# The recurrence's level products get a longer planned margin behind the VectorE multiplications that they read

## The chip, the core and the metric

The kernel runs on one core of a Trainium2 chip. The metric is the device time of one execution in microseconds (us), as the median of several executions: 1126.6 us over 3 runs (1125.8 to 1126.96). The engines are named as in the profile: PE is TensorE (its weight loads are PEld), DVE is VectorE, ACT is ScalarE, POOL is GpSimd and SP is SyncE, whose queue issues the DMAs here.

## What is computed

One layer of a streaming encoder, on x of shape (1, 1024, 1024) in float32. Token mixing comes first: RMSNorm with an adaLN shift and scale, one input projection of 3072 columns, a convolution group (gate, causal depthwise convolution over 31 taps, group norm, swish), an HGRN2 group of 4 heads with a gated linear recurrence in chunks of 64, then an output projection, RMSNorm, a gate and the residual. Channel mixing follows: the same norm, an MLP of width 4096 with a squared ReLU, RMSNorm, gate and residual. The recurrence, to which the change belongs, is this:

```python
def step(state, inp):
    qb, kb, vb, lb_ = inp
    cum = jnp.cumsum(lb_, axis=2)
    diff = cum[:, :, :, None, :] - cum[:, :, None, :, :]
    decay = jnp.exp(jnp.where(causal[None, None, :, :, None], diff, -jnp.inf))
    att = jnp.einsum("bhtk,bhsk,bhtsk->bhts", qb, kb, decay)
    o = jnp.einsum("bhts,bhsv->bhtv", att, vb) + \
        jnp.einsum("bhtk,bhkv->bhtv", qb * jnp.exp(cum), state)
    ...
```

The kernel never forms a cumulative logarithm. It builds `att` by levels of doubling block size.

## The kernel before, in words

**Stages.** First the x tiles are normalised and transposed and three column groups of the input projection are multiplied (`pf` on PE). Then the rest of the input projection runs, column group after column group, in the order of the list `ORDER`: the conv gate (`ptG`), the gate of one head (`pj`), the conv value (`ptU`), the recurrence's v (`ptV`), and the other groups of the heads (`pj`). Each group is 48 or, for the transposed ones, 4 times 48 matmuls of 128x512. The output projection (`pout`), the MLP's up projection (`pup`) and its down projection (`al`, `be`) follow. Everything else is laid in between these large products: the heads, the convolution, the modulation vectors.

**A head.** `head_att` goes through seven levels, h = 1, 2, 4 up to 64. At a level PE multiplies blocks of K with blocks of Q into a PSUM tile named `pl` (for h = 1 it sums a prepared product against ones). Then DVE multiplies half of the columns of Q and half of those of K by the decay E of the neighbouring half block, and squares E up, so that Q, K and E fit the next level; the next level's `pl` product reads the new Q and K. After these DVE copies `pl` into the attention tile under a mask (`COPY_PREDICATED`, h up to 8), or ACT copies it (h from 16). There are four heads, so 28 `pl` products. Before the levels come two diagonal products (`pd`), after them transposes (`tn`), state products (`pS`), outputs (`po`) and their transposes (`pot`). The levels of head 0 stand among `ptG`, those of head 1 among `ptU`, those of heads 2 and 3 among the last `pj` and the first `pout`.

**What sets the order.** All instructions are recorded in one program order by a small planner, the class `Weave`. It keeps a planned clock for each engine and adds an assumed cost for each instruction. The large products are the main stream; every other job is a generator that yields the planned moment at which it wants to go on, and the planner resumes it when PE's planned clock has passed that moment. On the chip the planned clocks do not exist: each engine works its instructions off strictly in the recorded order and waits on semaphores. A product that stands too early in PE's order therefore stops all of PE. `after("V")` gives the planned end of DVE's last instruction plus a margin, EXTRA = 0.4 us unless another is given. `split` puts a subtraction on POOL or on DVE, whichever is planned to end sooner, so other planned moments can also move work between these two engines.

**Other names.** `mods_mid` builds modulation vectors: for each it loads eight tiles `in_wada_n` through two or three staging tiles and adds them up on DVE (`SCALAR_TENSOR_TENSOR s<-s,c_act,s`); `ffn_cols` then sums over partitions on PE (`pm`), `gate_rows` likewise (`pg`). `t_val` adds a bias to `ptU` on DVE, multiplies by the gate on POOL and writes the result to memory (`udram`). When all four parts are written, `conv_input` loads `in_toep` and reads `udram` back into the tile `wide`, and `conv_mm` issues the convolution's small products (`cv`, eight groups of 64).

Of the kernel before, what the change touches and what calls it, by code (L numbers as in the profile page):

```python
# [57 lines left out]
AHEAD, RES = 10, 3  # L58


CSTEP = 8
NEAR, EXTRA, LO_G, DLAT, DLAT0 = 1.0, 0.4, 0.5, 2.0, 2.0
XIDLE, HIDLE, WIDLE = 0.3, 0.3, 0.3
XRANK, MRANK, RMODS, RCONV, RLOAD, RNORM = 0, 1, 7, 6, 3.5, 1.5
# [144 lines left out]
class Weave:  # L209
# [30 lines left out]
    def after(self, key, extra=None):  # L240
        return max(self.t[key], self.now) + (EXTRA if extra is None else extra)
# [47 lines left out]
def block_kernel(ctx: ExitStack, tc: tile.TileContext, x, vecs, masks, rows, vrow, crow, wada_t, wada_n,  # L289
# [3 lines left out]
    V = wv.engine(nc.vector, "V", lambda op, n: 0.16 + n / 930)  # L293
# [5 lines left out]
    after, idle = wv.after, wv.idle  # L299
# [12 lines left out]
    def free(tiles):  # L312
        for t in tiles:
            t.release()
# [24 lines left out]
    def ps1(name):  # L339
        return aux.take(psum.tile([P, 512], F32, tag="aux", bufs=2, name=name))  # L340
# [375 lines left out]
    def conv_mm(p, w, toeps):  # L716

        for q in range(2):
            yield acc.free
            ps = acc.take(ps_acc("cv"))  # L720
            for i in range(16):
                m = 16 * q + i
                for c in range(4):
                    for r in range(2):
# [3 lines left out]
                                  start=True, stop=True, us=0.0125)  # L728
                if i % CSTEP == CSTEP - 1:
                    yield wv.now + 0.5  # L730
# [95 lines left out]
    def head_q(j, ps):  # L826
        hd = heads[j]
        yield room(2 + HRES)
        q, Q = hd["q"], hd["Q"] = new(), new()
        A.activation(q.f, ps, AF.Sigmoid, bias=bcol(8 + j))  # L830
        yield after("A")
        V.scalar_tensor_tensor(q.f, ps, bcol(8 + j), q.f, ALU.add, ALU.mult)
        mm.done(ps, "V")
        yield hd["fk"]
        V.tensor_tensor(Q.f, q.f, hd["f"].f, ALU.mult)


        K = hd["K"].f
        yield idle("G", 1.0)
        G.tensor_tensor(q.f, q.f, K, ALU.mult)  # L840
        yield after("G", 0)
        yield room(3 + HRES)
        own = pair()
        prev = new(F32R)
        yield from split(q.f, own[0].r, own[1].r)
        Kv = K.rearrange("p (m s) -> p m s", s=2)
        Qv = Q.f.rearrange("p (m s) -> p m s", s=2)
        yield idle("G", 1.0)
        G.tensor_tensor(q.f[:, H0], Kv[:, :, 0], Qv[:, :, 1], ALU.mult)
        yield after("G", 0)  # L850
        yield from split(q.f[:, H0], prev.r[:, H0], prev.r[:, H1])
        hd["own"], hd["prev"] = own, prev
        q.release()
        wv.add(head_att(j), 1)

    def head_att(j):
        yield lambda: att_turn[0] >= j - 1
        hd = heads[j]
        att = atts[j % 2]
        f, K, Q = (hd[n].f for n in "fKQ")  # L860
        for half in range(2):
            yield aux_free
            pd = ps1("pd")
            for i, t in enumerate(hd["own"]):
                TE.matmul(pd, lhsT=ones_r, rhs=t.r[:, HALF[half]], start=(i == 0), stop=(i == 1))
            yield after("PE", 0.1)
            V.copy_predicated(att[:, half * 4:half * 4 + 4, :],
                              eye_u[:, None, :].broadcast_to([P, 4, P]),
                              pd.rearrange("p (n t) -> p n t", t=P))
            done1(pd, "V")  # L870
        free(hd["own"])
        h = 1
        while h <= 64:
            m = T // (2 * h)
            nb = 64 // h
            Qv = Q.rearrange("p (m s i) -> p m s i", s=2, i=h)
            Kv = K.rearrange("p (m s i) -> p m s i", s=2, i=h)

            Ev = f.rearrange("p (m s i) -> p m s i", s=2, i=h)[:, :, :, 0]
            yield aux_free  # L880
            pl = ps1("pl")
            av = att.rearrange("p n (b s i) -> p n b s i", s=2, i=h)
            Qn = Q.rearrange("p (n b s i) -> p n b s i", n=NT, s=2, i=h)
            plv = pl.rearrange("p (n b i) -> p n b i", n=NT, i=h)
            if h == 1:
                for i in range(2):
                    TE.matmul(pl, lhsT=ones_r, rhs=hd["prev"].r[:, HALF[i]], start=(i == 0), stop=(i == 1))
                hd["prev"].release()
            for n in range(NT if h > 1 else 0):
                if h in MASKED:  # L890
                    for g in range(4):
                        o = g * 32
                        TE.matmul(pl[o:o + 32, n * 16:(n + 1) * 16], lhsT=K[:, n * P + o:n * P + o + 32],
                                  rhs=Qn[:, n, g * nb // 4:(g + 1) * nb // 4, 1, :], start=True, stop=True, us=0.015)
                else:
                    for b in range(nb):
                        o = b * 2 * h
                        TE.matmul(plv[o:o + h, n, b, :], lhsT=K[:, n * P + o:n * P + o + h],
                                  rhs=Qn[:, n, b, 1, :], start=True, stop=True, us=h * 0.001)
            yield after("PE", 0.1)  # L900
            V.tensor_tensor(Qv[:, :, 1, :], Qv[:, :, 1, :],
                            Ev[:, :, 0:1].broadcast_to([P, m, h]), ALU.mult)
            V.tensor_tensor(Kv[:, :, 0, :], Kv[:, :, 0, :],
                            Ev[:, :, 1:2].broadcast_to([P, m, h]), ALU.mult)
            V.tensor_tensor(Ev[:, :, 0], Ev[:, :, 0], Ev[:, :, 1], ALU.mult)
            t = after("V")
            if h in MASKED:
                mk = lev_u[h].rearrange("p (b i) -> p b i", i=h)
                if h == 1:
                    V.copy_predicated(av[:, :, :, 1, :],  # L910
                                      mk[:, None, :, :].broadcast_to([P, NT, nb, h]), plv)
                else:
                    plg = pl[:, 0:P].rearrange("p (n b i) -> p n b i", n=NT, i=h)
                    for g in range(4):
                        o, bs = g * 32, slice(g * nb // 4, (g + 1) * nb // 4)
                        V.copy_predicated(av[o:o + 32, :, bs, 1, :],
                                          mk[o:o + 32, None, bs, :].broadcast_to([32, NT, nb // 4, h]),
                                          plg[o:o + 32])
            else:
                for b in range(nb):  # L920
                    o = b * 2 * h
                    A.activation(av[o:o + h, :, b, 1, :], plv[o:o + h, :, b, :], AF.Copy)
            done1(pl, "V" if h in MASKED else "A")
            yield t
            h *= 2
        hd["att"] = True
        wv.add(head_state(j), 1)
# [49 lines left out]
    def head_state(j):  # L977
        hd = heads[j]
        yield lambda: all(("vh", s) in hd for s in range(4))
        v, f = hd["v"].f, hd["f"].f  # L980
        yield room(2)
        Kn = new()
        yield from to_nat(hd["K"].f, Kn.f)
        hd["K"].release()
        yield room(1)
        hd["S"] = new()
        St = hd["S"].f
        yield after("A")
        for half in range(2):
            yield aux_free  # L990
            pS = ps1("pS")
            for i in range(4):
                n = half * 4 + i
                if n < NT - 1:
                    sl = slice(n * P, (n + 1) * P)
                    TE.matmul(pS[:, i * P:(i + 1) * P], lhsT=Kn.f[:, sl], rhs=v[:, sl], start=True, stop=True)
            yield after("PE", 0.1)
            for i in range(4):
                n = half * 4 + i
                if n < NT - 1:  # L1000
                    sl = slice(n * P, (n + 1) * P)
                    nxt = St[:, (n + 1) * P:(n + 2) * P]
                    psl = pS[:, i * P:(i + 1) * P]
                    if n == 0:
                        V.tensor_copy(nxt, psl)
                    else:
                        V.scalar_tensor_tensor(nxt, St[:, sl], f[:, n * P:n * P + 1], psl, ALU.mult, ALU.add)
            done1(pS, "V")
        Kn.release()
        hd["f"].release()  # L1010
        yield after("V")
        for half in range(2):
            wv.add(head_out(j, half), 2)
# [931 lines left out]
```

## Time and profile before

| what | value |
|---|---|
| median of 3 runs | 1126.6 us |
| the profiled execution, its own time | 1126.3 us |
| its span in the trace | 1124.3 us |
| PE busy | 1083.6 us, 96% of the span |
| DVE busy | 719.3 us, 64% |
| ACT busy | 464.1 us, 41% |
| POOL busy | 299.4 us, 27% |
| mean granted PE clock | 0.992 |

The profiled execution is 2.0 us longer than the span of its trace and 0.3 us shorter than the median. In a row of a timeline stand the start, the duration, the engine, the line and operation, the output and the inputs, and the number of instructions merged into the row; the square bracket gives the time for which the engine stood idle before it and what ended that. Recorded helper lines hide where an instruction was written (all of PE's products have one line), so tiles' names tell the rows apart.

### The profile page before, as it was taken

What the parts mean: (1) busy time and instruction counts of PE and PEld (TensorE: products, weight loads), DVE (VectorE), ACT (ScalarE), POOL (GpSimd) and SP (SyncE); (2) the same over time, 40 slices, a digit from 0 to 9 for tenths busy, and PEclk for the clock granted to TensorE, in tenths of its full rate; (3) what the DMA queues carried; (4) which work ended last, traced back from release to release, by engine and by line L of the source; (5) the groups of instructions that cost most, each with busy time, mean ns of one, the idle gap of its engine ahead of it and who ended that gap; (6) DMA issues with size and microseconds to landing.
All of it is one profiled execution on the core that took longest, in us unless ns stands there. A gap on an engine that the chain in (4) does not pass through costs nothing.

```text
span 1124.3 us, 17080 instructions
## 1 busy us (share of the span) xinstructions
PE 1083.6 (96%) x7036; PEld 880.4 (78%) x7036; DVE 719.3 (64%) x762; ACT 464.1 (41%) x659; POOL 299.4 (27%) x199
## 2 busy tenths in 40 slices
PE   6999998999999989989999999999999999999997
PEld 2787877778877778868888888888888888888886
DVE  3537678238599961766666975333266969997952
ACT  6641311002456433567452334456643334354530
POOL 5121022003373430482101420134400001303511
PEclk8999999999999999999999999999999999999999
DMA  9524433837311402454679745315667957675711
GB/s 365 194 82 132 132 110 120 210 89 191 92 57 39 132 20 75 168 204 171 225 242 341 279 148 187 113 57 179 214 238 268 323 204 243 226 275 176 292 56 75
DMA packets 57101, 195.21 MB, mean 174 GB/s; under 512 B 6208, under 2 KB 10688, under 8 KB 56768
## 3 DMA queue, kind: packets, MB, share of 16 engines
q1 hardware_dynamic: 57024, 194.13, 50.8%
q8 instruction: 55, 0.90, 0.3%
q14 instruction: 22, 0.18, 0.0%
HBM read 158.39 MB, written 35.72 MB: 173 GB/s over the span
## 4 chain that ended last, share of the span: by engine, by line
PE 78%; DVE 8%; DMA 4%; POOL 4%; issue 2%; ACT 2%; SPq 1%; POOLq 0%; DVEq 0%; ACTq 0%
PE pup L1829 26%; PE al L1829 15%; PE be L1829 12%; DVE s L236 7%; PE pout L1829 5%; PE pj L1829 5%; PE ptV L1829 4%; PE pf L1829 3%; DMA s<-in_wada_n 2%; PE ptG L1829 2%; POOL s L236 2%; ACT s L236 1%; PE pm L1829 1%; PE po L1829 1%; PE pl L1829 1%
## 5 line engine op out<-in xcount | busy, mean ns | idle before, releaser
L236 DVE TENSOR_TENSOR s<-s,s 128x1024 fp32r<-128x1024 f32 (+3 forms) x339 | 422.0, 1283 | 84.1 <-ACT s L236 49.9
L236 ACT ACTIVATE s<-s 128x1024 fp32r<-128x1024 f32 (+2 forms) x313 | 300.9, 993 | 346.5 <-DVE s L236 208.4
L236 POOL TENSOR_TENSOR s<-s,s 128x1024 fp32r<-128x1024 f32 (+4 forms) x86 | 198.2, 2312 | 546.1 <-ACT s L236 461.7
L1829 PE MATMUL pup<-s,s 128*128 128x512 f32 x1344 | 308.1, 390 | 0.0
L1829 PEld LDWEIGHTS pup<-s,s 128*128 128x128 f32 x1344 | 251.5, 188 | 51.9
L1829 PE MATMUL al<-s,s 128*128 128x512 f32 x768 | 175.0, 389 | 0.0
L1829 PEld LDWEIGHTS al<-s,s 128*128 128x128 f32 x768 | 144.1, 188 | 30.3 <-DVE s L236 0.4
L1829 PE MATMUL be<-s,s 128*128 128x512 f32 x576 | 131.0, 389 | 0.0
L1829 PEld LDWEIGHTS be<-s,s 128*128 128x128 f32 x576 | 108.1, 188 | 22.5
L1829 PE MATMUL pj<-s,s 128*128 128x512 f32 x432 | 107.4, 397 | 2.2 <-issue 1.5
L1829 PE MATMUL pout<-s,s 128*128 128x512 f32 x384 | 94.9, 401 | 2.0 <-DVE s L236 2.0
L1829 PEld LDWEIGHTS pj<-s,s 128*128 128x128 f32 x432 | 78.9, 188 | 18.4 <-issue 1.7
L1829 PEld LDWEIGHTS pout<-s,s 128*128 128x128 f32 x384 | 71.6, 191 | 17.0 <-DVE s L236 2.4
L236 DVE TENSOR_TENSOR s<-pup,s 128x1024 f32<-128x1024 f32 x24 | 29.3, 1222 | 47.5 <-PE pup L1829 47.3
L236 DVE SCALAR_TENSOR_TENSOR s<-s,c_act,s 128x1024 f32<-128x1024 f32 x28 | 39.5, 1411 | 29.7 <-DMA s<-in_wada_n 29.6
L236 DVE SCALAR_TENSOR_TENSOR s<-pup,s 128x1024 f32<-128x1024 f32 x16 | 19.6, 1225 | 53.3 <-PE pup L1829 50.3
L1829 PE MATMUL ptV<-s,s 128*128 128x512 f32 x192 | 47.4, 407 | 0.0
L1829 PE MATMUL ptU<-s,s 128*128 128x512 f32 x192 | 46.1, 394 | 0.0
L1829 PE MATMUL ptG<-s,s 128*128 128x512 f32 x192 | 45.9, 394 | 0.0
L1829 PEld LDWEIGHTS ptV<-s,s 128*128 128x128 f32 x192 | 37.5, 197 | 8.2
L236 ACT ACTIVATE junk<-s 128x1024 bf16<-128x1024 f32 (+1 forms) x30 | 30.0, 998 | 31.6 <-DVE s L236 24.2
L1829 PEld LDWEIGHTS ptG<-s,s 128*128 128x128 f32 x192 | 35.6, 188 | 7.8 <-ACT s L236 0.3
(126 smaller groups left out, 804.3 us busy)
## 6 DMA issues: line engine op xcount, KB each, us to landing
s<-in_wdn SPq DMA_DIRECT2D x72, 512.0 KB
s<-in_wup SPq DMA_DIRECT2D x56, 512.0 KB
s<-in_wada_n SPq DMA_DIRECT2D x32, 512.0 KB
s<-in_x SPq DMA_DIRECT2D x16, 512.0 KB
s<-in_wada_t SPq DMA_DIRECT2D x16, 512.0 KB
u<-s SPq DMA_DIRECT2D x16, 512.0 KB
s<-u SPq DMA_DIRECT2D x16, 512.0 KB
s<-in_wint SPq DMA_DIRECT2D x12, 512.0 KB
```

The lines of the kernel that those rows point to most:

```text
L236: return op(*a, **k)
L1829: return self.te.matmul(out, lhsT=lhsT, rhs=rhs, **k)
```

## The change

The margin behind the three DVE multiplications of a level becomes a parameter of its own, LEXTRA = 1.0 us, in place of EXTRA = 0.4 us. The moment `t` is what the generator yields at the end of the level, before the next level's product is recorded.

```diff
-CSTEP = 8
+CSTEP, LEXTRA = 8, 1.0
 ...
             V.tensor_tensor(Ev[:, :, 0], Ev[:, :, 0], Ev[:, :, 1], ALU.mult)
-            t = after("V")
+            t = after("V", LEXTRA)
             if h in MASKED:
```

No instruction of the computation is added or removed, but the planner records another order. Three places show how.

On PE, head 1's `pl` products among the `ptU` matmuls (`s_1233` is its Q, `s_693` its K). Each piece of the difference stands at a fixed place of the `ptU` stream.

```order
 L1829 MATMUL ptU<-s_601,s_111 128x512
 L1829 MATMUL ptU<-s_600,s_112 128x512
-L1829 MATMUL pl<-s_1233,s_693 32x16 x32
 L1829 MATMUL ptU<-s_600,s_113 128x512
 L1829 MATMUL ptU<-s_601,s_113 128x512
```

This is the product of h = 2; it goes 6 `ptU` matmuls further back. Counted through, the numbers of `ptU` matmuls from the product of h = 1 to that of h = 2 and so on to h = 64 were 18, 18, 18, 18, 24, 18, and are now 24, 24, 18, 18, 18, 18. Head 0, among `ptG`, had 18, 24, 18, 18, 24, and now has 24, 24, 18, 24, 18 before its last product, which goes 6 back within `pj`.

On DVE, the same head from the masked copy of h = 1 on (`s_1218` or `s_1224` is a modulation vector, `s_1424` or `s_1417` the second of the four parts of the conv value, `s_692` is E). Before:

```order
L236 COPY_PREDICATED s_682<-msk,pl 128x512
L236 SCALAR_TENSOR_TENSOR s_1218<-s_245,c_act,s_1218 128x1024
L236 TENSOR_TENSOR s_1233<-s_1233,s_692 128x256x2
L236 TENSOR_TENSOR s_693<-s_693,s_692 128x256x2
L236 TENSOR_TENSOR s_692<-s_692 128x256
L236 COPY_PREDICATED s_682<-msk,pl 32x8x8x2 x4
L236 TENSOR_TENSOR s_1424<-ptU,s_675 128x1024
L236 TENSOR_TENSOR s_1233<-s_1233,s_692 128x128x4
L236 TENSOR_TENSOR s_693<-s_693,s_692 128x128x4
```

And now:

```order
L236 COPY_PREDICATED s_682<-msk,pl 128x512
L236 SCALAR_TENSOR_TENSOR s_1224<-s_245,c_act,s_1224 128x1024
L236 TENSOR_TENSOR s_1417<-ptU,s_675 128x1024
L236 TENSOR_TENSOR s_1233<-s_1233,s_692 128x256x2
L236 TENSOR_TENSOR s_693<-s_693,s_692 128x256x2
L236 TENSOR_TENSOR s_692<-s_692 128x256
L236 COPY_PREDICATED s_682<-msk,pl 32x8x8x2 x4
L236 SCALAR_TENSOR_TENSOR s_1224<-s_245,c_act,s_1224 128x1024
L236 TENSOR_TENSOR s_1233<-s_1233,s_692 128x128x4
```

The evacuation of `ptU`, after which POOL multiplies by the gate, stood before the multiplications of h = 4 and now stands before those of h = 2. Likewise the last evacuation of `ptU` stood behind head 1's last level and now stands before it.

On PE, the partition sum `pm` of the second modulation vector stood alone among the `ptV` matmuls:

```order
L1829 MATMUL ptV<-s_721,s_105 128x512
L1829 MATMUL ptV<-s_720,s_106 128x512
L1829 MATMUL pm<-ones,s_1218 128x1 x8
L1829 MATMUL ptV<-s_761,s_107 128x512
L1829 MATMUL ptV<-s_762,s_107 128x512
```

Now it stands between the first two groups of the convolution's products:

```order
L1829 MATMUL cv<-wide,s_1724 32x32 x2
L1829 MATMUL cv<-wide,s_1725 32x32 x2
L1829 MATMUL pm<-ones,s_1224 128x1 x8
L1829 MATMUL cv<-wide,s_1722 32x32 x2
L1829 MATMUL cv<-wide,s_1723 32x32 x2
```

The convolution itself moved forward: 168 matmuls (`ptU` 6, `ptV` 162) lay between head 1's last `pl` and the first `cv` group, and now 126 (`ptV` alone). From the first up projection on, PE's order is the same as before.

## The prediction

> **What bounds the kernel now.** I read the page's busy times first, then the waits of PE by what ended them, then PE's timeline around each wait.
>
> ```profile
> span 1124.3 us, 17080 instructions
> PE 1083.6 (96%) x7036; PEld 880.4 (78%) x7036; DVE 719.3 (64%) x762; ACT 464.1 (41%) x659; POOL 299.4 (27%) x199
> ```
>
> PE is busy for 1083.6 of 1124.3 us, and the change adds it no work. What can move is the 40.7 us in which PE stands idle, and the slices in which its clock is low. The largest cause is the one that the change addresses (total us, times, longest):
>
> ```profile
> PE pl L1829 <- DVE s L236: 10.2, 8, 2.7
> ...
> PE cv L1829 <- issue: 2.4, 1, 2.4
> ```
>
> So at most 10.2 us lie in the waits of `pl` themselves, 0.9% of the time. Here they stand one by one for heads 0 and 1, in PE's timeline:
>
> ```profile
> 98.83 0.73 PE L1829 MATMUL pl<-s,s 128*32 128x16 f32 x64 [1.43 <-DVE s L236]
> ...
> 162.32 0.73 PE L1829 MATMUL pl<-s,s 128*32 128x16 f32 x64 [0.22 <-DVE s L236]
> 173.90 0.73 PE L1829 MATMUL pl<-s,s 128*32 128x16 f32 x64 [1.52 <-DVE s L236]
> ...
> 186.82 0.70 PE L1829 MATMUL pl<-s,s 128*32 128x32 f32 x32 [1.58 <-DVE s L236]
> ...
> 191.76 1.15 PE L1829 MATMUL pl<-s,s 128*64 128x64 f32 x16
> ...
> 201.35 1.92 PE L1829 MATMUL pm<-ones,s 128*128 128x1 f32 x16 [1.43 <-DVE s L236]
> ```
>
> Why DVE is late is in its own timeline, beside POOL's:
>
> ```profile
> 96.20 1.28 DVE L236 SCALAR_TENSOR_TENSOR s<-s,c_act,s 128x1024 f32<-128x1024 f32 x1 [3.15 <-DMA s<-in_wada_n]
> ...
> 165.60 1.29 DVE L236 TENSOR_TENSOR s<-s,s 128x512 f32<-128x512 f32 x2
> ...
> 170.30 3.46 DVE L236 TENSOR_TENSOR s<-s,s 128x512 f32<-128x512 f32 x2
> ...
> 170.46 2.75 POOL L236 TENSOR_TENSOR s<-s,s 128x1024 f32<-128x1024 f32 x1 [16.15 <-DVE s L236]
> 183.21 3.46 DVE L236 TENSOR_TENSOR s<-s,s 128x512 f32<-128x512 f32 x2
> 183.38 2.75 POOL L236 TENSOR_TENSOR s<-s,s 128x1024 f32<-128x1024 f32 x1 [10.17 <-DVE s L236]
> 397.32 5.06 DVE L236 TENSOR_TENSOR s<-s,s 128x512 f32<-128x512 f32 x2 [1.48 <-PE pl L1829]
> ```
>
> Two causes. At 98.83 a modulation product waited for its DMA and stood ahead of the multiplications. At 173.90 and 186.82 the pair of multiplications took 3.46 us in place of 1.29, each time with a POOL product beside it, which starts when DVE has evacuated `ptU`.
>
> **The change, term by term.** The price of a PE step comes from a long undisturbed row, and the price of an idle stretch includes what the clock does after it:
>
> ```profile
> 301.84 19.33 PE L1829 MATMUL pj<-s,s 128*128 128x512 f32 x84
> ...
> 204.00:208.00 4.00, 4.00 (x12) 0.57 0.62 175
> ```
>
> A matmul costs 19.33/84 = 0.23 us: 6 are 1.4 us, 18 are 4.1, 24 are 5.5, 126 are 29.0. After the wait and the small products at 201.35 the granted clock (third number from the end of the window's row) was 0.57 for 4 us, which lost 4 x 0.43 = 1.7 us.
>
> *Head 0:* the product of h = 2 goes 6 `ptG` back, 1.4 us of cover for a wait of 1.43. DVE's end is fixed by the DMA, so nearly all goes: -1.4 (from -1.4 to 0).
>
> *Head 1:* 0.22, 1.52 and 1.58 are 3.3 us. The product of h = 2 goes back by 1.4 us. The `ptU` evacuation now stands before the multiplications of h = 2, so the POOL product falls on them: the slow pair now has 24 matmuls and the product's own 0.7 us as cover, 6.2 us, against the evacuation and 3.46 (4.7 us) behind a modulation product. The next slow pair is that of h = 16, with 4.1 + 0.7 us. I leave 0.5 us of waiting: -2.8 (from -3.3 to 0).
>
> *`pm` and the first convolution group:* the wait at 201.35 and its slow clock, 1.4 + 1.7 = 3.1 us, leave their place. But `pm` now stands between two `cv` groups that come 42 matmuls nearer to head 1's last `pl`. Is their input there? The chain before (DVE, then on SP's queue the first loads for the convolution and the last of the four reads into `wide`, two windows with DMA share and GB/s last, and the first `cv`):
>
> ```profile
> 196.44 1.21 DVE L236 TENSOR_TENSOR s<-ptU,s 128x1024 f32<-128x1024 f32 x1
> ...
> 204.77 1.92 SPq L236 DMA_DIRECT2D s<-in_toep  x4
> ...
> 209.03 0.30 SPq L710 DMA_DIRECT2D wide<-udram  x1
> ...
> 228.00:230.00 2.00, 2.00 (x10) 1.67 (x9) 0.00 (x0) 0.45 (x1) 0.00 (x0) 1.00 0.38 150
> 230.00:232.00 2.00, 2.00 (x10) 1.66 (x9) 0.00 (x0) 0.62 (x1) 0.00 (x0) 1.00 0.01 2
> ...
> 236.23 1.52 PE L1829 MATMUL cv<-wide,s 64*32 64x32 f32 x128
> ```
>
> From 196.44 to the end of all these loads it is at most 230 - 196.4 = 33.6 us. The eight loads for the convolution (8 x 512 KB = 4.2 MB) share it with 1 MB issued behind them: 5.2 MB from 204.8 to 230, 0.2 MB per us, by which the eight alone end near 225, or 28 us after 196.4. Now the evacuation stands before head 1's last level and its matmuls end when that level's `pl` starts. In the old clock that is 191.76, less 4.2 gained above, plus 1.4 for the six `ptU` now ahead: 189.0. The input lands between 217 (28 us) and 222.6 (33.6 us); `cv` is asked for at 189.0 + 1.1 + 29.0 = 219.1. PE waits 0 to 3.5 us there, or a little later in `pm`, whose last modulation product needs a tile loaded behind `wide` and 1.3 us of DVE. I take a wait of 2 us and half a slow slice, 0.9: it cancels the 3.1 leaving. Net 0 (from -3.1 to +3).
>
> *Convolution groups closer together:* the second `cv` group of the first pair stopped for 2.4 us (the `issue` row above: PE waited for nothing that the trace shows). In the second half of the convolution the pairs had 6 `pj` and a `po` or `pot` between them; now 6 `pj` alone. Bounds 0 and 2 x 2.4 = 4.9; I take +1.5, nearer to none because another pair with only 6 matmuls between lost next to nothing.
>
> *Heads 2 and 3 and what stands around them:*
>
> ```profile
> 322.23 0.66 PE L1833 MATMUL cpb<-msk,s 128*128 128x128 f32 x4 [1.05 <-DVE s L236]
> 330.61 0.72 PE L1829 MATMUL pd<-s,ones_r 128*128 128x512 f32 x2 [0.85 <-ACT s L236]
> 341.71 0.74 PE L1829 MATMUL pl<-s,s 128*32 128x16 f32 x64 [0.34 <-DVE s L236]
> 366.93 4.37 PE L1829 MATMUL pj<-s,s 128*128 128x512 f32 x18 [0.67 <-DVE s L236]
> 371.60 0.66 PE L1833 MATMUL tn<-msk,s 128*128 128x128 f32 x4 [0.30 <-DVE s L236]
> 385.01 0.74 PE L1829 MATMUL pl<-s,ones_r 128*128 128x512 f32 x2 [1.54 <-DVE s L236]
> 397.93 0.66 PE L1833 MATMUL pot<-msk,s 128*128 128x128 f32 x4 [0.67 <-ACT s L236]
> 404.05 0.73 PE L1829 MATMUL pl<-s,s 128*32 128x16 f32 x64 [2.70 <-DVE s L236]
> ...
> 304.00:404.00 100.00, 91.87 (x838) 73.36 (x836) 91.00 (x119) 52.11 (x94) 53.98 (x25) 1.00 0.22 69
> ```
>
> These waits are 8.1 us. Between head 2's levels stood 12 to 18 `pj` and a few transposes; now 18 to 24. Against that, DVE is busy for 91 of these 100 us (third pair of the last row), and the changed order gives it more: two subtractions of 128x1024 and three of 128x512 go over from POOL, and five of the eight modulation products of `gate_rows` that ran before 301 now come after the last `cv`:
>
> ```profile
> 88.76 1.23 DVE L236 TENSOR_TENSOR s<-s,s 128x1024 fp32r<-128x1024 f32 x1 [3.56 <-ACT s L236]
> ...
> 422.76 0.69 DVE L236 TENSOR_TENSOR s<-mfull,s 128x512 fp32r<-128x512 f32 x1 [1.37 <-ACT s L236]
> ```
>
> That is 2 x 1.23 + 3 x 0.69 + 5 x 1.28 = 10.9 us more for DVE, not all of it inside this stretch; but head 2's levels are spread over 138 `pj` in place of 90 (11 us) and the last `cv` comes 30 matmuls (6.9 us) earlier, so DVE has more time too. Queued behind each modulation product are the next level's multiplications, and PE waits for these. I take half of the waits as gone: -4.0 (from -8.1 to +4, if the extra DVE work shows on PE by a third).
>
> *The last `pot`:* both halves of head 3's outputs now come together right before the final 132 `pout`; half by half there were 12 `pout` between. What follows a `pot` is an evacuation on DVE, a copy on ACT and a subtraction on DVE:
>
> ```profile
> 420.64 0.75 DVE L236 SCALAR_TENSOR_TENSOR mfull<-pot,vec,s 128x512 f32<-128x512 f32 x1
> ...
> 422.11 0.62 ACT L236 ACTIVATE s<-mfull 128x512 fp32r<-128x512 f32 x1
> ```
>
> With the 0.69 us from above that is 2.1 us, of which 6 `pout` hide 1.4: about +0.5 (0 to 2).
>
> Sum: -1.4 - 2.8 + 0 + 1.5 - 4.0 + 0.5 = -6.2 us. The profiled execution took 1126.3 us (span 1124.3 and 2.0 around it), 0.3 below the median of 1126.6. So the median goes to 1126.6 - 6.2 = 1120.4 us.
>
> **The rivals.**
>
> *A. Forecast:* PE's waits shrink by 3 to 9.5 us, 1117 to 1123.5. Chance 0.55.
>
> *B. The slow pairs follow.* If POOL's products beside the multiplications are what counts, a margin of 0.6 us more does not reach the 2.2 us by which they lengthen a pair. The three waits behind such pairs (1.52, 1.58, 2.70: 5.8 us) stay somewhere; the sum is near -0.5, 1126. For it: the rows at 170.30, 183.21 and 397.32. Against it: planned moments fall between whole 6-matmul steps, so many levels got 5.5 us. Chance 0.17. The Trainium skill (SBUF — State Buffer, Who interferes with whom) speaks for this one: a VectorE instruction with two SBUF inputs contends with a GpSimd instruction that reads SBUF, and whichever issues first blocks the other. The rows agree (2.2 us lost beside a POOL product of 2.75).
>
> *C. The convolution waits for its input, slower.* Place: the first `cv` group. If the loads land no earlier than before, at 230, the wait is 230 - 219.1 = 10.9 us, and a slow slice of 1.7 follows, against 3.1 saved: +9.5, in sum +3.3, 1130. It decides from a wait of about 8 us on, where the whole gain is gone. For it: the DMA engines' share is still 0.38 in 228 to 230. Against it: the evacuation moves before the last level. Chance 0.10. On the slow slice, the Trainium skill (TensorE: Matmul & The Clock Gate, What's actually happening) says that the clock halves after an idle window of about 3.4 us that runs freely. By that rule a wait of 2 us need not cost a slice; the trace has both, a slow slice behind 201.35 and none behind the 2.70 us at 404.05.
>
> *D. DVE becomes the bound of heads 2 and 3.* The 10.9 us more do not fit into its 9 idle us: 8.1 stay and 4 come on top; in sum -6.2 + 8 = +1.8, 1128.4. Chance 0.10.
>
> *E. Everything hides:* all of 1.4, 3.3, 3.1 and 8.1 less 1.0 new waits, 1126.6 - 15 = 1112, or half way there, 1115. Chance 0.08.
>
> **How the numbers follow.** A change of this kernel can be told from none at about 0.2%, 2.25 us: below 1124.3 is faster, above 1128.9 slower. A and E are faster, and a little of B: 0.67. The rest of B and half of D are the same: 0.19. C and the other part of D, with a stop that no row names: 0.14. The range takes A whole, B, most of D, and E down to its middle: 1115 to 1128.5.
>
> **What would show it.** In the changed trace the waits of `pl` for DVE should fall from 10.2 us to about 3. The 98.83 wait should be gone, the pairs of 3.46 us still there but under cover. PE should wait up to 2 us at the first `cv` or at `pm`, and a second `cv` of a pair may stop for 2 us. DVE in the 100 us of heads 2 and 3 should be as full as before. I am wrong if the waits of `pl` stay at 8 us or more (B or D), or if `cv` waits 8 us (C), or if a new wait stands where none did, above all at `pd`, `pot` or the first `pout`.

## The result: 0.9% slower, not faster

| | us |
|---|---|
| before, median of 4 runs | 1126.2 (1124.6 to 1127.0) |
| changed, median of 4 runs | 1136.9 (1135.4 to 1139.2) |
| ratio | 1.009, 95% interval 1.0071 to 1.0108 |
| predicted | 1120.4 (1115 to 1128.5) |

The sign of the prediction was wrong and the time lies outside its range. Of the runs further down, low_on_vector has one execution of 1348.2 us at a granted clock of 0.751 among its five, which its ratio leaves out.

The page of the changed kernel, its first lines and then the waits of PE by cause (total us, times, longest):

```profile
span 1137.4 us, 17080 instructions
PE 1090.3 (96%) x7036; PEld 886.2 (78%) x7036; DVE 725.3 (64%) x767; ACT 464.0 (41%) x659; POOL 285.0 (25%) x194
```

```profile
PE pl L1829 <- DVE s L236: 14.5, 9, 4.2
...
PE cv L1829 <- DMA wide<-udram: 4.9, 1, 4.9
...
PE cv L1829 <- issue: 1.0, 1, 1.0
```

PE ran the same 7036 products, but was busy for 6.7 us longer (1090.3 against 1083.6): they ran at a lower clock, 0.982 on the mean against 0.992. The waits of `pl` grew from 10.2 to 14.5 us. The profiled execution is the longest of the changed kernel's four, 2.4 us above their median, so its span shows 13.1 us more where the medians show 10.7. Where the 13.1 us went follows from the first start of a few tiles in both traces, which cut the program at places that both share:

| stretch | before | changed | difference |
|---|---|---|---|
| up to the first `ptV` (heads 0 and 1) | 194.3 | 193.0 | -1.3 |
| (the same from the first `pl` on) | 101.8 | 99.0 | -2.8 |
| first `ptV` to first `tn` (convolution) | 59.2 | 62.2 | +2.9 |
| first `tn` to first `pup` (heads 2 and 3) | 247.1 | 258.8 | +11.7 |
| first `pup` to the end | 623.6 | 623.4 | -0.2 |

Heads 0 and 1 did gain. The third stretch holds the loss; here it is in the view of windows (length, then busy time of PE, PEld, DVE, ACT and POOL, the granted clock, the DMA share and GB/s), before and then changed:

```profile
253.60:500.70 247.10, 233.34 (x2201) 191.94 (x2200) 172.95 (x237) 114.86 (x247) 110.50 (x73) 0.99 0.33 103
```

```profile
255.20:514.00 258.80, 239.27 (x2200) 196.46 (x2199) 176.74 (x238) 114.84 (x247) 100.31 (x69) 0.97 0.31 95
```

PE's idle time rose from 13.8 to 19.5 us (length less busy time), +5.8, and the same products took 5.9 us longer at the lower clock. PE's timeline of the changed kernel names the stops, and windows of 4 us show the clock behind them:

```profile
351.15 1.06 PE L1829 MATMUL pl<-s,s 128*32 128x16 f32 x64 [4.16 <-DVE s L236]
373.12 0.77 PE L1829 MATMUL pl<-s,s 128*32 128x32 f32 x32 [1.90 <-DVE s L236]
384.15 1.22 PE L1829 MATMUL pl<-s,ones_r 128*128 128x512 f32 x2 [3.55 <-DVE s L236]
...
409.14 0.69 PE L1829 MATMUL pl<-s,s 128*16 128x16 f32 x64 [1.51 <-DVE s L236]
```

```profile
348.00:352.00 4.00, 0.85 (x64) 0.88 (x64) 3.71 (x7) 0.18 (x1) 0.26 (x1) 0.71 0.00 0
352.00:356.00 4.00, 4.00 (x24) 3.20 (x17) 3.52 (x6) 0.45 (x1) 0.00 (x0) 0.50 0.18 28
...
372.00:376.00 4.00, 2.88 (x37) 2.48 (x38) 3.97 (x6) 3.26 (x5) 0.53 (x1) 0.70 0.38 125
376.00:380.00 4.00, 4.00 (x17) 3.18 (x17) 4.00 (x3) 2.16 (x3) 4.00 (x2) 0.87 0.47 120
...
384.00:388.00 4.00, 3.85 (x14) 2.87 (x15) 3.69 (x6) 0.00 (x0) 0.00 (x0) 0.59 0.48 142
```

The products that stopped are head 2's h = 4 and h = 32 and head 3's h = 1 and h = 16. Before the change there was one stop among head 2's levels, of 0.34 us. DVE and POOL of the changed kernel show why the first one is late:

```profile
339.78 0.74 DVE L236 SCALAR_TENSOR_TENSOR mfull<-pot,vec,s 128x512 f32<-128x512 f32 x1
341.21 0.69 DVE L236 TENSOR_TENSOR s<-mfull,s 128x512 fp32r<-128x512 f32 x1 [0.70 <-ACT s L236]
343.17 5.64 DVE L236 TENSOR_TENSOR s<-s,s 128x1024 fp32r<-128x1024 f32 x3 [1.26 <-ACT s L236]
...
349.24 1.76 DVE L236 COPY_PREDICATED s<-msk,pl 32x128 f32<-32x128 uint32 x4
...
376.13 5.09 DVE L236 TENSOR_TENSOR s<-s,s 128x512 f32<-128x512 f32 x2
381.14 2.32 DVE L236 TENSOR_TENSOR s<-s 128x16 f32<-128x16 f32 x1
```

```profile
343.59 1.90 POOL L236 TENSOR_SCALAR s<-s 128x1024 f32<-128x1024 f32 x1
345.47 2.79 POOL L236 TENSOR_TENSOR s<-s,s 128x1024 fp32r<-128x1024 f32 x1
...
375.47 7.95 POOL L236 TENSOR_TENSOR s<-s,s 128x1024 fp32r<-128x1024 f32 x3 [3.65 <-ACT s L236]
```

The row at 343.17 merges a low-part subtraction of `split` (128x1024), which waited 1.26 us for ACT, with the two multiplications of h = 2 that are queued behind it. A clean pair takes 1.29 us and the subtraction 1.2, 2.5 in all; these took 5.64, beside two POOL instructions. The masked copy of h = 2, queued behind them, was late by as much: it ended at 351.00, and the product of h = 4 started at 351.15. At 376.13 head 2's last pair took 5.09 us, and the squaring behind it, 128x16, 2.32, both beside three POOL subtractions.

So five theories went to the chip. **H**: the margin in heads 2 and 3 is the loss. **C**: the early convolution is, through what it shifts. **Q**: the place of the multiplications in DVE's queue. **B**: POOL's subtractions beside them. **K**: the clock that each stop lowers.

### The profile page after: what moved, and what is told of

Same layout as the page of the kernel before. It is cut to its first block, busy times and chain, and to the rows that moved or that the text cites. A ratio compares the mean times of both kernels' runs of the same rounds, so it can differ in the third digit from the quotient of the medians.

```text
span 1137.4 us, 17080 instructions
## 1 busy us (share of the span) xinstructions
PE 1090.3 (96%) x7036; PEld 886.2 (78%) x7036; DVE 725.3 (64%) x767; ACT 464.0 (41%) x659; POOL 285.0 (25%) x194
## 4 chain that ended last, share of the span: by engine, by line
PE 76%; DVE 9%; DMA 6%; POOL 4%; ACT 2%; issue 2%; SPq 1%; POOLq 0%; DVEq 0%; ACTq 0%
PE pup L1829 26%; PE al L1829 15%; PE be L1829 11%; DVE s L236 9%; PE pj L1829 5%; PE pout L1829 4%; DMA s<-in_wada_n 4%; PE pf L1829 3%; POOL s L236 2%; PE ptU L1829 2%; PE pm L1829 1%; PE ptV L1829 1%; ACT s L236 1%; PE po L1829 1%; PE pl L1829 1%
## 5 line engine op out<-in xcount | busy, mean ns | idle before, releaser
L236 DVE TENSOR_TENSOR s<-s,s 128x1024 fp32r<-128x1024 f32 (+4 forms) x341 | 428.2, 1293 | 83.0 <-ACT s L236 53.7
L236 POOL TENSOR_TENSOR s<-s,s 128x1024 fp32r<-128x1024 f32 (+4 forms) x84 | 192.8, 2302 | 568.1 <-ACT s L236 456.7
L1829 PE MATMUL pup<-s,s 128*128 128x512 f32 x1344 | 308.1, 390 | 0.0
L1829 PEld LDWEIGHTS pup<-s,s 128*128 128x128 f32 x1344 | 251.6, 188 | 51.8
L1829 PE MATMUL al<-s,s 128*128 128x512 f32 x768 | 175.0, 389 | 0.0
L1829 PEld LDWEIGHTS al<-s,s 128*128 128x128 f32 x768 | 144.1, 188 | 30.3 <-DVE s L236 0.4
L1829 PE MATMUL be<-s,s 128*128 128x512 f32 x576 | 131.0, 389 | 0.0
L1829 PEld LDWEIGHTS be<-s,s 128*128 128x128 f32 x576 | 108.1, 188 | 22.4
L1829 PE MATMUL pj<-s,s 128*128 128x512 f32 x432 | 111.8, 409 | 0.0
L1829 PE MATMUL pout<-s,s 128*128 128x512 f32 x384 | 95.3, 401 | 3.2 <-DVE s L236 2.7
L1829 PEld LDWEIGHTS pj<-s,s 128*128 128x128 f32 x432 | 82.0, 196 | 17.2
L1829 PEld LDWEIGHTS pout<-s,s 128*128 128x128 f32 x384 | 71.5, 191 | 18.7 <-DVE s L236 3.4
L236 DVE SCALAR_TENSOR_TENSOR s<-s,c_act,s 128x1024 f32<-128x1024 f32 x28 | 36.9, 1319 | 32.4 <-DMA s<-in_wada_n 32.2
L1829 PE MATMUL ptV<-s,s 128*128 128x512 f32 x192 | 46.0, 400 | 0.0
L1829 PE MATMUL ptG<-s,s 128*128 128x512 f32 x192 | 45.9, 394 | 0.0
L1829 PE MATMUL ptU<-s,s 128*128 128x512 f32 x192 | 45.7, 393 | 0.0
L1829 PEld LDWEIGHTS ptV<-s,s 128*128 128x128 f32 x192 | 36.7, 193 | 7.9
L1829 PEld LDWEIGHTS ptG<-s,s 128*128 128x128 f32 x192 | 35.6, 188 | 7.7 <-ACT s L236 0.3
```

What stands on the lines that cost most here:

```text
L236: return op(*a, **k)
L1829: return self.te.matmul(out, lhsT=lhsT, rhs=rhs, **k)
```

## The experiments

All times stand against the kernel before, run on the same chip beside them.

| run | median us | ratio to before, 95% interval |
|---|---|---|
| heads01 | 1125.8 | 0.9993 (0.9977 to 1.0010) |
| heads23 | 1128.1 | 1.0016 (0.9998 to 1.0034) |
| conv_hold | 1127.2 | 1.0013 (0.9994 to 1.0031) |
| one_long | 1132.9 | 1.0045 (1.0025 to 1.0066) |
| fill | 1143.6 | 1.0160 (1.0125 to 1.0195) |
| fill_spare | 1133.1 | 1.0068 (1.0046 to 1.0091) |
| no_pool_sub | 1118.2 | 0.9920 (0.9895 to 0.9945) |
| before_no_pool_sub | 1119.6 | 0.9939 (0.9917 to 0.9961) |
| margin12 | 1122.6 | 0.9963 (0.9945 to 0.9981) |
| margin14 | 1123.1 | 0.9971 (0.9957 to 0.9984) |
| low_on_vector | 1120.3 | 0.9939 (0.9919 to 0.9959) |
| m04_low_on_vector | 1121.1 | 0.9951 (0.9930 to 0.9972) |
| m12_low_on_vector | 1115.6 | 0.9906 (0.9883 to 0.9929) |

### Which heads, and the convolution

```diff
-            t = after("V", LEXTRA)
+            t = after("V", LEXTRA if j < 2 else EXTRA)      # heads01
+            t = after("V", EXTRA if j < 2 else LEXTRA)      # heads23
```

```diff
-            yield wv.t["S"] + 2 * DLAT
+            yield wv.t["S"] + 2 * DLAT + (0 if p else 6.0)  # conv_hold
```

> The longer margin stands in heads 0 and 1 alone; heads 2 and 3 are placed with the old 0.4 us. Up to head 2 the order is the changed kernel's, so the convolution still stops for its input (4.90 us) and its clock gap stays. Theory H (the loss comes from where the products of heads 2 and 3 now stand: pl waits of 4.16, 1.90, 3.55 and 1.51 us and the clock gaps behind them): some 10 us better than the changed kernel, 1125 to 1129 us. Rival C (the early convolution shifted everything behind it, and that is what spoils heads 2 and 3): still 1134 to 1138 us, with pl waits over 3 us left.

> The longer margin stands in heads 2 and 3 alone; heads 0 and 1 and the convolution are the kernel's before. Theory H: the loss is here, 1134 to 1138 us. Rival C: the time of before, 1124 to 1128 us, or a little less, because the convolution stands where it stood.

> The changed kernel, with the first convolution asked for 6 us later in the plan, so that 6 us more of ptV stand ahead of it. Theory C: the 4.90 us wait and the half clock behind it (about 5 us) go, and the shift behind it too: 1125 to 1130 us. Theory H: the convolution's own share alone, at most 8 us, if heads 2 and 3 keep their waits: 1129 to 1134 us. Neither holds if the time stays at 1136 us with the wait gone.

heads01 came to 1125.8 us, inside H's range, although its convolution still stopped (first waits of PE, then its third stretch):

```profile
PE pl L1829 <- DVE s L236: 7.9, 8, 3.1
...
PE cv L1829 <- DMA wide<-udram: 3.6, 1, 3.6
```

```profile
251.30:500.60 249.30, 236.45 (x2200) 194.65 (x2199) 174.40 (x239) 115.08 (x247) 97.59 (x68) 0.98 0.31 99
```

249.3 us against 258.8: the loss is in the orders of heads 2 and 3, as H has it, and C falls as the main cause. But heads23, with the long margin only there, lost 1.6 us on the median, not the 8 to 12 that H asked for. And conv_hold, with the long margin everywhere, took 1127.2 us. That lies in the range of C, but not by C's mechanism: its convolution stretch was no shorter (61.9 us; in place of `cv`, a `pm` waited for 4.2 us), while heads 2 and 3, which fell into yet another order, took 248.9. The margin in heads 2 and 3 is thus not bad by itself. Something in the one order that 1.0 us makes there is.

### One swap in VectorE's queue

```diff
-            t = after("V", LEXTRA if j < 2 else EXTRA)
+            t = after("V", LEXTRA if j < 2 or (j, h) == (2, 1) else EXTRA)
```

> The kernel of heads01 (old margin in heads 2 and 3) with the long margin at one place more: after the multiplications of head 2, h=1, so that the product of h=2 is placed 0.6 us later. Nothing else is asked to move, but VectorE's queue then holds the 128x1024 subtraction that waits for ScalarE ahead of the multiplications of h=2 and not behind them. Theory Q (the loss starts at this swap: the multiplications then wait for ScalarE, 1.26 us, for the subtraction, 1.36 us, and run beside GpSimd): the product of h=4 waits 3.5 to 4.5 us as in the changed kernel against 0.35 us in heads01, with a clock gap of some 3 us behind it, and the run takes 5 to 9 us more than heads01, 1130 to 1135 us. Rival N (the loss of heads 2 and 3 is spread over their levels and this one swap is not its start): within 2 us of heads01, 1124 to 1128 us.

The order on DVE against that of heads01, at the place meant (`s_527` is the low part, `s_2952`, `s_2825` and `s_2824` are head 2's Q, K and E):

```
 L236 TENSOR_TENSOR s_2640<-mfull,s_2639 128x512
+L236 TENSOR_TENSOR s_527<-s_775,s_526 128x1024
 L236 TENSOR_TENSOR s_2952<-s_2952,s_2824 128x256x2
 L236 TENSOR_TENSOR s_2825<-s_2825,s_2824 128x256x2
 L236 TENSOR_TENSOR s_2824<-s_2824 128x256
 L236 COPY_PREDICATED s_681<-msk,pl 32x8x8x2 x4
-L236 TENSOR_TENSOR s_527<-s_775,s_526 128x1024
```

DVE's timeline there, in heads01 and then in one_long:

```profile
338.21 0.69 DVE L236 TENSOR_TENSOR s<-mfull,s 128x512 fp32r<-128x512 f32 x1 [0.70 <-ACT s L236]
338.82 1.29 DVE L236 TENSOR_TENSOR s<-s,s 128x512 f32<-128x512 f32 x2
340.02 0.63 DVE L236 TENSOR_TENSOR s<-s 128x256 f32<-128x256 f32 x1
340.56 1.81 DVE L236 COPY_PREDICATED s<-msk,pl 32x128 f32<-32x128 uint32 x4
342.41 1.36 DVE L236 TENSOR_TENSOR s<-s,s 128x1024 fp32r<-128x1024 f32 x1
```

```profile
336.95 0.69 DVE L236 TENSOR_TENSOR s<-mfull,s 128x512 fp32r<-128x512 f32 x1 [0.70 <-ACT s L236]
338.91 5.64 DVE L236 TENSOR_TENSOR s<-s,s 128x1024 fp32r<-128x1024 f32 x3 [1.27 <-ACT s L236]
344.48 0.59 DVE L236 TENSOR_TENSOR s<-s 128x256 f32<-128x256 f32 x1
```

In heads01 the pair starts as soon as DVE is free, takes 1.29 us and is done before POOL's next subtraction begins; the low part comes behind. In one_long the pair stands behind the low part and waits for what that waits for, and then meets POOL: 5.64 us again. The product of h = 4 on PE, in heads01 (where the expectation's 0.35 us belongs to the next product, that of h = 8) and, with the stops that followed, in one_long:

```profile
342.52 0.73 PE L1829 MATMUL pl<-s,s 128*32 128x16 f32 x64 [0.18 <-DVE s L236]
```

```profile
346.90 1.06 PE L1829 MATMUL pl<-s,s 128*32 128x16 f32 x64 [4.19 <-DVE s L236]
367.93 1.07 PE L1829 MATMUL pl<-s,s 128*32 128x32 f32 x32 [3.27 <-DVE s L236]
401.15 0.90 PE L1829 MATMUL pl<-s,s 128*32 128x16 f32 x64 [3.39 <-DVE s L236]
```

It stops for 4.19 us against 0.18. The run took 7.1 us more than heads01 on the medians (5.9 by the ratios, since the kernel before took 0.7 us longer beside it), as Q had asked, and its third stretch took 258.5 us, 9.2 more. N falls. Q as stated is what happened at this place. It is not the whole distance: the planner goes on from another state after the swap, so later rows moved too, and two more stops of over 3 us followed.

### The subtractions on GpSimd

```diff
+            if 1 <= att_turn[0] <= 3:
+                G.memset(lo.bitcast(F32), 0.0)
+            else:
                 G.tensor_tensor(lo, src, hi.bitcast(F32), ALU.subtract)
```

> The changed kernel in the same order on every engine, but from the first product of head 2 to the end of head 3 GpSimd's subtractions that form low parts (11 of 128x1024 and one of 128x512) are memsets to zero, which read nothing: the low parts of these weights and of part of the mix are left out. Theory B (GpSimd beside the level multiplications makes them late: pairs of 4.28 and 5.09 us against 1.29): the pairs take 1.3 to 1.5 us, the waits of 4.16, 1.90 and 3.55 us fall to 1.3, 0.6 and 1 or less, and with the clock gaps behind them 6 to 10 us come back: 1127 to 1131 us. Rival Q alone (the place in VectorE's queue decides, not the contention): the first wait stays at 2.5 us or more and the time at 1133 us or more.

> The control to no_pool_sub: the kernel before, with GpSimd's low-part subtractions from head 2's first product to the end of head 3 made memsets to zero (the low parts are left out). no_pool_sub came to 1118.2 us, 18.6 less than the changed kernel. Theory B (the order of the changed kernel loses because more of its multiplications run beside these subtractions): without them the two orders are about equal, so 1115 to 1121 us here, a gain of 6 to 11 us. Rival Q alone (the loss is the place in VectorE's queue, whatever GpSimd does): the distance between the two orders stays, about 1107 to 1111 us here.

Ten subtractions of 128x1024 and one of 128x512 were replaced in the changed kernel, in an order that is otherwise its own, and ten of 128x1024 and four of 128x512 in the kernel before. Its third stretch without them, then that of the kernel before without them:

```profile
250.70:493.30 242.60, 233.51 (x2200) 192.53 (x2199) 160.72 (x238) 114.72 (x247) 81.68 (x69) 0.99 0.33 102
```

```profile
252.90:496.80 243.90, 234.54 (x2201) 193.27 (x2200) 158.23 (x237) 115.32 (x248) 89.02 (x76) 0.99 0.33 106
```

The two orders are then equal: 242.6 and 243.9 us, 1118.2 and 1119.6 us on the medians. With the subtractions they are 11.7 us apart. So the order loses nothing by itself, and Q alone falls. B holds for the cause; its price was too low, since 18.6 us came back where it had asked for 6 to 10. That POOL itself was late is no rival: PE's only wait for POOL in this stretch is one of 2.04 us at `pt`, in both kernels. One point I had not expected. The subtractions lengthen DVE's work about as much in both kernels: 172.95 - 158.23 = 14.7 us before, 176.74 - 160.72 = 16.0 us in the changed one. Only the price differs: 3.2 us of time before (247.1 against 243.9) and 16.2 in the changed kernel (258.8 against 242.6), in one trace each; on the medians it is 6.5 and 18.6 us. Of the 16.2 us, 10.4 are idle time of PE and 5.8 its busy time at the lower clock.

Groups by shape over the third stretch show which instructions took the delay. The level multiplications before, with the subtractions and without, then the same of the changed kernel with two of its squares of E (L1829 and L1832 are one and the same helper line of PE):

```profile
L236 DVE TENSOR_TENSOR s<-s,s 128x512 f32<-128x512 f32 x28 | 27.0, 1005 | 13.1 <-PE pl L1829 13.0
L236 DVE TENSOR_TENSOR s<-s,s 128x512 f32<-128x512 f32 x28 | 20.3, 766 | 17.5 <-PE pl L1832 17.5
```

```profile
L236 DVE TENSOR_TENSOR s<-s,s 128x512 f32<-128x512 f32 x28 | 30.5, 1132 | 10.0 <-PE pl L1829 10.0
L236 DVE TENSOR_TENSOR s<-s 128x64 f32<-128x64 f32 x2 | 2.7, 1354 | 0.0
L236 DVE TENSOR_TENSOR s<-s 128x16 f32<-128x16 f32 x2 | 2.5, 1251 | 0.0
L236 DVE TENSOR_TENSOR s<-s,s 128x512 f32<-128x512 f32 x28 | 22.4, 840 | 10.7 <-PE pl L1829 10.7
```

The multiplications lost 6.7 us before and 8.1 in the changed kernel. The squares of 128x64 and 128x16 lost 1.1 before (2.0 against 0.9 us) and 4.3 in the changed kernel (5.2 against 0.9). So these steps of the levels, which stand ahead of what PE waits for, lost 7.8 us before and 12.4 in the changed kernel. DVE's own low-part subtractions of 128x1024 turn the other way: they lost 3.2 us before (25.1 against 21.9) and 1.7 in the changed kernel (24.3 against 22.6). This shift of 4.6 us goes the right way and is smaller than the difference in price; that the rest lies in which level had time to spare is argued from the stops and not counted. Without POOL's subtractions the same three instructions as at 343.17 take 3.47 us, and head 2's last pair and its square are clean:

```profile
336.46 3.47 DVE L236 TENSOR_TENSOR s<-s,s 128x1024 fp32r<-128x1024 f32 x3 [1.26 <-ACT s L236]
...
363.77 1.28 DVE L236 TENSOR_TENSOR s<-s,s 128x512 f32<-128x512 f32 x2
364.97 0.18 DVE L236 TENSOR_TENSOR s<-s 128x16 f32<-128x16 f32 x1
...
366.31 1.28 DVE L236 TENSOR_TENSOR s<-s,s 128x512 f32<-128x512 f32 x2
```

The wait for ACT, 1.26 us, is still there; the product of h = 4 then stops for 1.23 us in place of 4.16.

### The clock behind the stops

```diff
+            for _ in range(FILL.get((j, h), 0)):
+                nc.tensor.matmul(pl, lhsT=ones_r, rhs=ones_r[:, None, :].broadcast_to([P, 4, P]),
+                                 start=True, stop=True)      # fill_spare: into an idle bank
```

> The changed kernel in the same order, with matmuls that compute nothing (128x512 on a constant, written to the bank that the real product then overwrites) in the five longest stops: 20 ahead of the first convolution, 16, 7, 14 and 5 ahead of the products of head 2 h=4 and h=32 and head 3 h=1 and h=16. They take the place of the waits and add no time of their own as long as they are shorter than these. Theory K (half of the loss is the clock that each stop lowers; the granted clock cost 11.5 us more in the changed kernel, (1-0.982)*1137.4 against (1-0.992)*1124.3): the clock stays near 1.00 in 340 to 394 us and the run is 7 to 11 us shorter than the changed kernel, 1126 to 1130 us. Rival (only the waits cost, the clock follows the small products and not the stops): the same slices stay at 0.5 to 0.9 and the time stays at 1136 to 1138 us.

> The changed kernel in the same order, with matmuls that compute nothing again in the stops, this time sized by the 389 ns that one took in the first such run (9, 3, 7 and 2 in heads 2 and 3, 10 ahead of the convolution: 3.5, 1.2, 2.7, 0.8 and 3.9 us, each shorter than its stop) and, in heads 2 and 3, written to the idle accumulator bank, so that they do not wait for the bank of the product. Theory K (each stop's length is doubled by the clock it lowers): granted clock 1.00 from 340 to 394 us, the run 5 to 8 us shorter than the changed kernel, 1129 to 1132 us. Rival: the clock gaps stay and the time is 1136 to 1138 us.

The edit of fill has a flaw. Its products went into the tile of the product behind them, and waited for that bank themselves:

```profile
PE pl L881 <- DVE s L236: 5.1, 1, 5.1
PE pl L887 <- DVE s L236: 4.2, 1, 4.2
```

They ran after the stops, not in them, and the run tells nothing on K. It tells something else. These products read neither Q nor K, yet those ahead of head 2's h = 4 waited for 4.17 us, where the real product had waited for 4.16, and those ahead of head 3's h = 1 for 5.13. So these two stops end when a masked copy has emptied a PSUM bank, and not when the multiplications are done; the copies (of `pl` and of `pd`) are queued behind late multiplications. Ahead of head 2's h = 32 the products that compute nothing ran without a wait, and the real one behind them still waited for DVE.

In fill_spare the products do not wait. They are shorter than its expectation says: the 20 of fill at the convolution started from 219.4 to 223.8 us, one every 0.23 us, and 389 ns is one's duration, which overlaps with the next. So 2.1, 0.7, 1.6 and 0.5 us of the stops in heads 2 and 3 were filled. The clock then stayed at 1.00 in all the slices named above, yet the third stretch came out at 256.8 us, only 2.0 less:

```profile
248.30:505.10 256.80, 239.00 (x2223) 196.47 (x2221) 176.78 (x238) 114.91 (x247) 100.39 (x69) 0.99 0.31 97
```

Of the 239.0 busy us some 4.8 are the 21 fillings, so the real products took 234.2, 5.1 less than in the changed kernel. But idle time and fillings together are 17.8 + 4.8 = 22.6 us against 19.5: head 3's first product stopped for 3.49 us behind 1.6 of filling, where it had been 3.55. PE arrived earlier and waited longer for DVE. K's gap is real in the rows and was mostly time that DVE would have taken anyhow; K's 5 to 8 us did not come (3.8 on the median, 2.5 by the ratios, part of it at the convolution, whose stretch was 57.9 us).

### The margin as a number, and a better kernel

```diff
-CSTEP, LEXTRA = 8, 1.0
+CSTEP, LEXTRA = 8, 1.2      # margin12;  1.4 in margin14
```

> The changed kernel with a margin of 1.2 us in place of 1.0. If the margin as such costs (products placed later are worse placed), it is no better than the changed kernel, 1136 to 1140 us. If the loss is one unlucky order in VectorE's queue (theory Q), another order falls out and the time can come back to 1124 to 1130 us.

> A margin of 1.4 us. If times between 1122 and 1137 us are a scatter of orders (0.4: 1126, 1.0: 1137, 1.2: 1123), it lies anywhere in that span; if a longer margin helps once the unlucky order of 1.0 is passed, 1119 to 1124 us; if it costs by later products, over 1130 us.

With 0.4, 1.0, 1.2 and 1.4 us the times are 1126, 1137, 1123 and 1123. The first stretch gains steadily, counted from the first `pl` to the first `ptV`: 101.8 us at 0.4, 97.3 to 99.0 in the eight traces with 1.0, 94.6 and 94.5 at 1.2 and 1.4. The third is a scatter of orders: 247.1, 258.8, 250.7 and 254.8. So 1.0 us is one unlucky order. The result at 1.4 fits both the scatter and a margin that helps; two more values do not tell these apart.

The last three kernels compute everything and move the sharing of low parts in heads 2 and 3 towards DVE; the whole order is planned anew.

```diff
-        if max(wv.t["G"], wv.now) + ... <= max(wv.t["V"], wv.now) + 0.16 + n / 930 + LO_G:
+        if max(wv.t["G"], wv.now) + ... <= max(wv.t["V"], wv.now) + 0.16 + n / 930 + (LO_G if not 1 <= turn <= 3 else -2.0):
```

(`turn` counts the heads whose outputs are placed; -2.0 with a margin of 1.0 us in low_on_vector; -1.0 with 1.2 in m12_low_on_vector; -9.0, which leaves POOL none, with 0.4 in m04_low_on_vector.)

> The changed kernel, whole computation, with the rule that shares out the low-part subtractions shifted by 2.5 us towards VectorE while heads 2 and 3 are at work (LO_G 0.5 to -2.0): the order after head 1 falls out anew and GpSimd keeps 8 subtractions less. Theory B: fewer pairs run beside GpSimd, though VectorE has 1.36 us more to do for each: 1124 to 1131 us. Rival D (VectorE is the bound of heads 2 and 3, 85 to 92% busy there): each subtraction moved costs its own time, 1138 us or more.

> Margin 1.2 us with the rule for the subtractions shifted by 1.5 us towards VectorE in heads 2 and 3 (GpSimd keeps 5 or so less). margin12 came to 1122.6 us with one stop of 5.16 us left at head 3. Theory B: 1117 to 1122 us. Rival D: 1123 to 1130 us.

> The old margin of 0.4 us, whole computation, with the low-part subtractions of heads 2 and 3 all given to VectorE. If the gain of low_on_vector (1120.3 us) and m12_low_on_vector (1115.6 us) comes from the subtractions alone (theory B, the margin worth nothing by itself): 1115 to 1121 us. If the longer margin brings the 5 to 6 us that the prediction gave it once the contention is gone: 1122 to 1126 us here.

All three are faster than the kernel before; the one with 1.2 us is the best of the study at 1115.6 us, 0.9906 (0.9883 to 0.9929). The third stretch of low_on_vector and of m04_low_on_vector:

```profile
251.60:495.00 243.40, 233.54 (x2202) 192.59 (x2200) 172.23 (x245) 114.71 (x247) 81.72 (x62) 0.99 0.31 100
```

```profile
252.40:494.60 242.20, 233.11 (x2209) 192.78 (x2201) 171.38 (x251) 115.39 (x247) 77.24 (x59) 0.99 0.34 104
```

That is what the memsets gave (242.6 and 243.9), with nothing left out, and DVE is no busier than before (172.95), because what it takes over costs about what the contention cost. A rival D, that DVE cannot carry these subtractions, falls. Two of the three came out below B's ranges, and m04_low_on_vector at the upper end of its own. The margins 0.4 and 1.0 are not told apart here (1121.1 and 1120.3 us), so the 5 to 6 us that the prediction gave the longer margin do not show even without the contention: 2.6 us gained up to the first `ptV` (98.9 against 101.5 from the first `pl`) are lost again, 1.8 at the convolution and 1.2 in the third stretch. Between these and 1.2 lie 5 us. They come from the first two stretches (94.4 us from the first `pl` against 98.9 in low_on_vector, and 56.7 against 60.0 at the convolution); the third stretch is longer, 246.4 us.

## Why the prediction was wrong, step by step

**Heads 0 and 1, -1.4 and -2.8: right.** Predicted -4.2 together; the profiled execution shows -2.8 and the seven others with the same order up to the first `ptV` -2.9 to -4.4. PE's waits for DVE there fell from 5.6 to 3.4 us. The wait at 98.83 fell from 1.43 to 0.28 us, 1.52 to 0.45, and 1.58 went; one that I had not foreseen, 1.60 us, came at head 0's h = 16. The list of waits in the prediction leaves out one, 0.89 us at 157.30 ahead of head 1's first product; it stayed, at 0.88.

**The convolution, 0 and +1.5: the wait was under-sized and the second term did not come.** I took 2 us of waiting (0 to 3.5) from an input that lands 28 to 33.6 us after the evacuation. It landed 34.9 us after it (192.05 to 226.98) and PE waited 4.90 us, in the four other traces with this order and no filling 2.6 to 3.6; `pm` waited another 0.61. The stretch from the first `ptV` to the first `tn` lost 2.9 us in the profiled execution and 0.0 to 1.9 in those four, inside the bounds of -3.1 to +3. The +1.5 for groups closer together was not seen: the pairs of the second half ran without a stop, and the stop in the first half fell from 2.44 to 0.98 us. Rival C's price (a wait of 8 us or more) did not come.

**Heads 2 and 3, -4.0 (-8.1 to +4), and the last `pot`, +0.5: this step failed.** The stretch that holds both lost 11.7 us. The last `pot` has little part in that: 0.85 us in two waits for ACT (0.34 and 0.51), inside its bounds. The waits were to fall by half; those of `pl` for DVE in this stretch rose from 4.6 to 11.1 us, and the lower clock cost another 5.9. I counted the cover, 18 to 24 matmuls in place of 12 to 18, and DVE's extra work, and set one against the other. What I did not do is to follow where the margin puts the multiplications themselves. They are recorded right behind the level's product; a product that is placed later takes them with it, to a later place in DVE's queue, behind whatever was recorded in between. In head 2 that was a subtraction that waits for ACT, and behind it the pair met POOL. I also took the multiplications alone as what PE waits for, and not the masked copy behind them that frees the bank. The upper bound of +4 let the extra work show by a third; it had no term for more of the contention falling on the steps of the levels (12.4 us against 7.8), nor for the clock behind each stop.

**Rival B** had the right cause, POOL beside the multiplications, and the wrong size: I let it eat the gain (1126) and not cost 16.2 us in place of 3.2. The Trainium skill (SBUF — State Buffer, Who interferes with whom) adds that a GpSimd instruction that only writes does not contend with a VectorE instruction with two SBUF inputs. The traces agree: a memset of POOL ran from 366.33 to 367.29 us beside the pair at 366.31 above, which took 1.28.

```profile
366.33 0.96 POOL L236 MEMSET s<- 128x1024 f32 x1 [2.27 <-PE pj L1829]
```

**Rival D** said that DVE would become the bound of heads 2 and 3. What was shown is that DVE's lateness, by contention, holds PE up, and not the 10.9 us of moved work. Without POOL's subtractions DVE is only 2.5 us busier in the stretch than before (160.72 against 158.23), and where those subtractions are given to DVE outright, the stretch is short.

**The marks set beforehand** worked: `pl` waits of 8 us or more were to mean B or D, and they were 14.5. The chance of slower, 0.14, was too small, since I gave the failed step bounds that reached further down than up with no reason for it.

**Still open:** why about the same delay of DVE costs 13 us more in one order, beyond the 4.6 us counted above and the stops shown; and how much of one_long's 7.1 us is the swap itself and how much what the planner did after it; an order that differs from the changed kernel's at that one place alone was not tried.

## What to carry to other kernels

When a margin or a due time moves an instruction in one engine's order, follow what is recorded behind it on the other engines: it moves along, and its new neighbours in that queue set the price. Before judging such a number, look for contention that makes the outcome depend on the order, take it away first, and then compare settings; a single value is one sample of a scatter that was 14 us wide here. The same contention cost 3 us in one order and 16 in the other (6.5 and 18.6 on the medians). And count the cover of a product up to the last thing that it waits for, the copy that frees its bank included.

## What the runs showed of the hardware

- In the changed kernel a stop of 1.90 us ahead of 373.12 was followed by slices at 0.70 and 0.87 of the clock, while one of 2.70 us ahead of 404.05 in the kernel before was followed by none (1.00 from 404 to 408 us). The Trainium skill (TensorE: Matmul & The Clock Gate, What's actually happening) puts the drop after an idle window of about 3.4 us that runs freely; a stop of 1.90 us would not fill one, so the length of the stop alone does not tell it here.
- In fill_spare, keeping the clock up with products that compute nothing gave 5.1 us of PE time back and 3.1 of it went into longer waits for VectorE.
- A VectorE instruction of 128x16 elements that takes 0.18 us alone took 2.32 us beside GpSimd subtractions of 128x1024 (the row at 381.14 of the changed kernel): the delay went by the neighbour, not by its own size.
